# A two-layer trunk: layer 1's output projection as a seven-product stage behind the attention, and layer 0's weight sums and norm factors issued sooner

## The chip, the cores and the metric

One core of one Trainium2 chip runs the whole program. The metric is the device time of one execution in microseconds; the kernel before takes 1605.94 us, the median of three runs (1605.65 to 1606.53).

## What is computed

```python
def reference(x, norm_g, pool_w_in, pool_w, pool_scale, pool_w_out, sb_w_in, sb_w_out, norm_f):
    h = x                                        # (1, 1024, 1024) float32
    u = rms_norm(h, norm_g[0])                   # layer 0: pooling mixer
    xb, z = split(u @ pool_w_in, 2)              # 2048 channels each, 4 groups of 512
    pooled = [trailing_mean(xb[g], w) - xb[g] for g, w in enumerate((2, 4, 8, 16))]
    y = concat(pooled[g] @ pool_w[g]) * pool_scale * silu(z)
    h = h + y @ pool_w_out
    u = rms_norm(h, norm_g[1])                   # layer 1: stick-breaking attention
    q, k, v, z = split(u @ sb_w_in)              # 16 heads, q and k of 64, v of 128 columns
    a[t, s] = sigmoid(z_ts) * prod_{s<j<t} (1 - sigmoid(z_tj)),  s < t
    h = h + (concat(a @ v) * silu(z)) @ sb_w_out
    return rms_norm(h, norm_f)
```

All of it is float32. `sb_w_out` is 2048 x 1024.

## The kernel before

**Arithmetic.** Every float32 operand of a matmul is split into a high and a low part (`split`, L93: ACT copies the high part, DVE subtracts, L98 and L99), and a product is three matmuls (`mm3`, L87 to L91: high x high, high x low, low x high). `raw_of` (L102) loads an operand of 128 x 512 on SP's queue.

**Layer 0.** The input projection, and later the output projection, multiply 2 x 2 blocks of matrices with seven products instead of eight. That needs sums of blocks: sums of the weights on POOL (`sums`, L218), of the input on DVE, and of the results where the banks are read. `first_w` and the products `c1`, `c2` start it; `factors` (L176) loads the rows of x in 512 KB tiles, squares them on ACT and makes the root of the norm on POOL; `spread` (L187) turns it with PE and copies it; `to_u` (L195) scales x with it on DVE. Then four channel groups follow (`gi`, with windows of 2, 4, 8, 16). In each, `Group.rest` (L244) makes the branch and the gate in seven products, `pool_block` (L287) the window sums on DVE (L294, L297), and `mixed` (L305) the group's own matmul, the gate, and the y blocks: POOL puts y and its sums into DRAM (L321, L333 to L337). `out_sums` (L226) makes one of eight jobs of the output projection's weights: it loads four blocks into `a_raw` tiles (six buffers, which `Group.load` shares), adds four times on POOL, and puts four sums into DRAM from POOL's queue (L231, L233). The output projection is a stage of its own: `out_product` (L125) does one of its products in 8 blocks of 12 matmuls.

**Layer 1.** The attention goes by head, and in a head by slots of 256 queries. A slot's chain is: scores on PE (L714, L715), sigmoids on ACT (L719, L720), a mask on POOL (L723), a running product on DVE (L726), a product on DVE (L730), another mask on POOL (L733), transposes on PE (L758), splits on ACT and DVE (L761, L762), and the sum with v on PE; at the end of a query block DVE multiplies the gate in (L784). Between these steps `dense()` issues filler: pieces of the projections of q and k, z and v of the next heads (`qk_item`, `z_item`, `v_item`), and of the output projection (`out_item`, `out_proj`, L565). `QUANTA` and `order` say what is due in which head, and `rate` spreads it over the head's steps. The output projection takes a pair of heads at a time, with all eight products of blocks: for each of 8 row tiles and 2 column halves 6 matmuls over the pair, and an addition into `h` on DVE (L572). The last pair follows at the end, and `finish` (L674) makes the final norm of each row tile: two squares on ACT, three small steps on POOL (L115 to L119), two multiplications on DVE (L686), and the store.

**Order.** The program is written engine-neutral; a scheduler then sets the order of the instructions on each engine by its own estimate of their times, and tile pools hand out buffers, with waits where a buffer's last use is not over. What stands where on an engine is therefore read from the order, not from the code.

Of the kernel before, what the change touches and what calls it, by code (L numbers as in the profile page):

```python
# [15 lines left out]
P = 128  # L16
S = 1024
# [28 lines left out]
def trunk(ctx, tc, x, xt, g, pw, pg, psc, pwo, sqk, sv, sz, swo, nf, out):  # L46
# [38 lines left out]


# [53 lines left out]
    with tc.tile_pool(name="l0", bufs=2) as l0:  # L140
# [22 lines left out]

        def load_xt(k, l, n):
# [233 lines left out]
        firsts = [[xb_tile() for _ in range(2)], [l0.tile([P, S], F32, name="t0") for _ in range(2)]]  # L398
# [17 lines left out]

        for gi in range(len(WINDOWS)):
            pooled = {}
            for cp in range(2):
                if gi + cp:  # L420
                    dst = [xb_tile("old" if gi == 0 and i else "xb", 2 - (gi == 0 and i)) for i in range(2)]
                    Group(gi * 4 + 2 * cp).rest(dst, AF.Copy)
                    if gi > 1 and cp == 0:
                        out_sums((0, 7)[gi - 2])
# [4 lines left out]
            for op in range(2):  # L429
# [9 lines left out]
                if gi + op:  # L439
                    dst = [l0.tile([P, S], F32, name="t0") for _ in range(2)]  # L440
# [3 lines left out]
                if 0 < 2 * gi + op < 7:  # L444
# [9 lines left out]
    slots_ = ctx.enter_context(tc.tile_pool(name="slots", bufs=48, reuse_waits="tile"))  # L454
# [9 lines left out]


    with tc.tile_pool(name="ob", bufs=4, reuse_waits="tile") as ob:
        def operands(n):

            i, j = {1: (0, 0), 2: (0, 1), 4: (1, 1)}.get(n, (0, 0))

            def of(kb):
                w = wd[n][kb] if n in wd else pwo[8 * j + kb][:, i * 512:i * 512 + 512]
                return split(raw_of(w, ob)), split(raw_of(yd[n][kb], ob, "y_raw"), ob, "y")
# [5 lines left out]

        def rows(l):  # L480
            return range(4 * HALVES[l], 4 * HALVES[l] + 4)

        add = nc.gpsimd.tensor_tensor

        def masked(t, n, ps):
            if t < NT - 1:
                nc.vector.tensor_tensor(h[t, n], ps, h[t, n], ALU.add)
            else:
                nc.vector.scalar_tensor_tensor(
                    h[t, n], in0=ps, scalar=but_first, in1=h[t, n], op0=ALU.mult, op1=ALU.add)  # L490
# [69 lines left out]
    ps_d = ctx.enter_context(tc.tile_pool(name="ps_d", bufs=3, space=PSUM, reuse_waits="tile"))  # L560
    ps_q = ctx.enter_context(tc.tile_pool(name="ps_q", bufs=2, space=PSUM, reuse_waits="tile"))
    ps_t = ctx.enter_context(tc.tile_pool(name="ps_t", bufs=2, space=PSUM, reuse_waits="tile"))
    ps_o = ctx.enter_context(tc.tile_pool(name="ps_o", bufs=1, space=PSUM, reuse_waits="tile"))

    def out_proj(ys, w4, t):  # L565

        for n in range(2):
            po = ps_d.tile([P, 512], F32, name="pd")
            for i, (yh, yl) in enumerate(ys):
                wh, wl = w4[2 * i + n]  # L570
                mm3(po, yh, yl, wh, wl, i == 0, i == 1)
            nc.vector.tensor_tensor(h[t, n], po, h[t, n], ALU.add)  # L572


    with tc.tile_pool(name="l1", bufs=1, reuse_waits="tile") as l1:
        def load_w(*srcs):

            return [split(raw_of(src[:, c:c + 512], l1, bufs=4))
# [3 lines left out]
        qk, vt, gt, yt = {}, {}, {}, {}  # L582
# [27 lines left out]
        def z_item(head, halves=(1, 0)):  # L610
            w2 = load_w(sz[head])
            yield
            for half in halves:
# [7 lines left out]
                t1 = l1.tile([P, 512], F32, name="t1", bufs=4)  # L621
# [31 lines left out]
        o_w = {}  # L653

        def out_item(pr, pieces, last=False):
            if pr not in o_w:
                o_w[pr] = load_w(swo[2 * pr], swo[2 * pr + 1])
                yield
            for m in pieces:
                for tt in range(2):  # L660
                    ts_ = slice(tt * P, (tt + 1) * P)
                    ys = [(yt[2 * pr + a, m][0][:, ts_], yt[2 * pr + a, m][1][:, ts_]) for a in range(2)]
                    out_proj(ys, o_w[pr], 2 * m + tt)
                    if last:
                        finish(2 * m + tt)
                    yield

        nfb = []
        late_rows = []
        LATE_T = 6  # L670
        ended = []
        ov = out.rearrange("(t p) c -> t p c", p=P)

        def finish(t):  # L674
            if not nfb:
                for n in range(2):
                    b = l1.tile([P, 512], F32, name="w_raw", bufs=4)
                    nc.sync.dma_start(b, nf[:, n * 512:n * 512 + 512].broadcast_to([P, 512]))
                    nfb.append(b)
            if t < LATE_T and not ended:  # L680
                late_rows.append(t)
                return
            rs = rstd_of([h[t, 0], h[t, 1]])
            for n in range(2):
                cs = slice(n * 512, n * 512 + 512)
                nc.vector.scalar_tensor_tensor(  # L686
                    h[t, n], in0=h[t, n], scalar=rs, in1=nfb[n], op0=ALU.mult, op1=ALU.mult)
# [241 lines left out]
```

## Time and profile before

| | |
|---|---|
| median of three runs | 1605.94 us |
| the profiled execution, its own time | 1603.79 us |
| its span on the core | 1602.1 us |
| PE busy | 1545.7 us (96%) |
| DVE busy | 1135.7 us (71%) |
| ACT busy | 662.8 us (41%) |
| POOL busy | 412.5 us (26%) |
| mean granted clock of TensorE | 0.985 |
| chain that ended last | PE 72%, DVE 7%, DMA, ACT and POOL 1% each |

The span is cut in three: up to about 464 us layer 0's projection and pooling, to 633 us its output projection and the norm of layer 1, then the attention to 1583 us and the end. Times are of one profiled execution. An engine's busy time says little by itself: matmuls overlap, so a matmul's own length is longer than the step from one to the next.

### The profile page before, as it was taken

What the parts mean: (1) busy time and instruction counts of PE and PEld (TensorE: products, weight loads), DVE (VectorE), ACT (ScalarE), POOL (GpSimd) and SP (SyncE); (2) the same over time, 40 slices, a digit from 0 to 9 for tenths busy, and PEclk for the clock granted to TensorE, in tenths of its full rate; (3) what the DMA queues carried; (4) which work ended last, traced back from release to release, by engine and by line L of the source; (5) the groups of instructions that cost most, each with busy time, mean ns of one, the idle gap of its engine ahead of it and who ended that gap; (6) DMA issues with size and microseconds to landing.
All of it is one profiled execution on the core that took longest, in us unless ns stands there. A gap on an engine that the chain in (4) does not pass through costs nothing.

```text
span 1602.1 us, 23391 instructions
## 1 busy us (share of the span) xinstructions
PE 1545.7 (96%) x8256; PEld 1325.5 (83%) x8256; DVE 1135.7 (71%) x1681; ACT 662.8 (41%) x1310; POOL 412.5 (26%) x903
## 2 busy tenths in 40 slices
PE   7899999988989998999999999999999999999997
PEld 6677888866778886989889889889889889889886
DVE  6976957969945676477757757747757757757678
ACT  7432322212335464454435435435434434434444
POOL 0336465586440121111101101101101101101113
PEclk9899999998999998999999999999999999999999
DMA  8124352463468562111021021021021021021112
GB/s 309 33 69 156 105 184 103 149 222 138 147 242 294 183 200 72 56 57 41 27 66 41 27 66 40 27 66 40 28 66 41 27 66 40 28 66 40 33 42 106
DMA packets 75125, 149.92 MB, mean 94 GB/s; under 512 B 9728, under 2 KB 9728, under 8 KB 75008
## 3 DMA queue, kind: packets, MB, share of 16 engines
q1 hardware_dynamic: 67184, 123.25, 23.8%
q0 software_dynamic: 7680, 25.17, 4.2%
q8 instruction: 65, 1.06, 0.3%
q14 instruction: 52, 0.43, 0.1%
q10 hardware_dynamic: 144, 0.01, 0.0%
HBM read 110.64 MB, written 29.36 MB: 87 GB/s over the span
## 4 chain that ended last, share of the span: by engine, by line
PE 72%; DVE 7%; issue 1%; DMA 1%; ACT 1%; POOL 1%; SPq 0%; DVEq 0%; POOLq 0%; ACTq 0%
PE pd L89 15%; PE pd L91 15%; PE pd L90 15%; PE bk L89 4%; PE bk L90 4%; PE bk L91 4%; PE pt L758 4%; PE po L89 2%; PE po L90 2%; PE po L91 2%; PE pq L714 2%; PE pq L715 2%; DVE wsum L294 2%; DVE w_lo L99 1%; DVE wsum L297 1%
## 5 line engine op out<-in xcount | busy, mean ns | idle before, releaser
L726 DVE TENSOR_TENSOR_SCAN om<-om 128x257 f32<-128x257 f32 (+1 forms) x192 | 187.1, 979 | 80.3 <-POOL om L723 34.5
L99 DVE TENSOR_TENSOR w_lo<-w_raw,w_hi 128x512 fp32r<-128x512 f32 x214 | 157.0, 741 | 86.6 <-ACT w_hi L98 82.5
L89 PE MATMUL pd<-slot,w_hi 128*128 128x512 f32 x512 | 202.8, 396 | 4.1 <-DVE slot L542 4.0
L90 PE MATMUL pd<-slot,w_hi 128*128 128x512 f32 x512 | 201.7, 394 | 0.0
L91 PE MATMUL pd<-slot,w_lo 128*128 128x512 f32 x512 | 200.4, 392 | 0.0
L98 ACT ACTIVATE w_hi<-w_raw 128x512 fp32r<-128x512 f32 x214 | 133.6, 627 | 159.8 <-PE pd L90 75.9
L719 ACT ACTIVATE om<-pq 128x256 f32<-128x256 f32 (+1 forms) x192 | 94.4, 492 | 167.7 <-PE pq L715 161.9
L89 PE MATMUL pd<-w_hi,slot 128*128 128x256 f32 x512 | 146.4, 286 | 0.0
L723 POOL TENSOR_SCALAR_AFFINE_SELECT om<-om 128x128 f32<-128x128 f32 x128 | 49.2, 387 | 375.4 <-ACT om L719 373.1
L91 PE MATMUL pd<-w_hi,slot 128*128 128x256 f32 x512 | 144.5, 282 | 0.0
L90 PE MATMUL pd<-w_lo,slot 128*128 128x256 f32 x512 | 144.2, 282 | 0.0
L98 ACT ACTIVATE w_hi<-a_raw 128x512 fp32r<-128x512 f32 x88 | 53.7, 627 | 150.6 <-PE bk L90 57.4
L89 PEld LDWEIGHTS pd<-slot,w_hi 128*128 128x128 f32 x512 | 96.7, 189 | 22.4 <-DVE slot L542 4.3
L762 DVE TENSOR_TENSOR at_l<-pt,at_h 128x512 fp32r<-128x512 f32 (+1 forms) x160 | 99.6, 626 | 21.1 <-ACT at_h L761 20.8
L91 PEld LDWEIGHTS pd<-slot,w_lo 128*128 128x128 f32 x512 | 96.8, 189 | 19.9 <-DVE w_lo L99 0.4
L761 ACT ACTIVATE at_h<-pt 128x512 fp32r<-128x512 f32 (+1 forms) x160 | 86.7, 552 | 63.9 <-PE pt L758 63.2
L90 PEld LDWEIGHTS pd<-slot,w_hi 128*128 128x128 f32 x512 | 96.8, 189 | 18.1
L730 DVE TENSOR_TENSOR om<-pq,om 128x256 f32<-128x256 f32 (+1 forms) x192 | 104.8, 551 | 9.1 <-DVE om L726 0.5
L89 PE MATMUL pd<-w_hi,y_h 128*128 128x512 f32 x256 | 107.0, 418 | 0.4 <-ACT y_h L787 0.4
L90 PE MATMUL pd<-w_lo,y_h 128*128 128x512 f32 x256 | 102.2, 399 | 0.0
L91 PE MATMUL pd<-w_hi,y_l 128*128 128x512 f32 x256 | 100.4, 395 | 0.0
L718 POOL MEMSET om<- 128x1 f32 x192 | 18.0, 99 | 315.2 <-PE pt L758 210.1
(315 smaller groups left out, 4088.7 us busy)
## 6 DMA issues: line engine op xcount, KB each, us to landing
a_raw<-in_pw SPq DMA_DIRECT2D x64, 256.0 KB, 3.3
y_raw<-y_dram SPq DMA_DIRECT2D x52, 256.0 KB, 3.1
y_dram<-t POOLq DMA_DIRECT2D x48, 256.0 KB, 2.9
a_raw<-in_pwo SPq DMA_DIRECT2D x36, 256.0 KB, 2.7
w_raw<-in_sqk SPq DMA_DIRECT2D x34, 256.0 KB, 2.7
w_raw<-in_sz SPq DMA_DIRECT2D x34, 256.0 KB, 3.0
w_raw<-w_dram SPq DMA_DIRECT2D x32, 256.0 KB, 2.9
w_raw<-in_sv SPq DMA_DIRECT2D x32, 256.0 KB, 2.7
```

Of the source, the lines that this page charges most:

```text
L89: nc.tensor.matmul(ps, lhsT=lh, rhs=rh, start=start, stop=False, skip_group_check=more)
L90: nc.tensor.matmul(ps, lhsT=lh, rhs=rl, start=False, stop=False, skip_group_check=more)
L91: nc.tensor.matmul(ps, lhsT=ll, rhs=rh, start=False, stop=stop, skip_group_check=more)
L98: act(hi, raw, AF.Copy)
L99: nc.vector.tensor_tensor(lo, raw, hi, ALU.subtract)
L719: act(om[:, 1:1 + n], pz, AF.Sigmoid, scale=-ZSCALE)
L723: nc.gpsimd.affine_select(out=om[:, 1:1 + P], in_=om[:, 1:1 + P], pattern=[[1, P]], base=0, channel_multiplier=-1, compare_op=ALU.is_gt, f ...
L726: nc.vector.tensor_tensor_scan(out=om[:, :1 + n], data0=om[:, :1 + n], data1=om[:, :1 + n], initial=1.0 if s.first else carry[r], op0=ALU. ...
L730: nc.vector.tensor_tensor(om[:, :n], pz, om[:, :n], ALU.mult)
L758: nc.tensor.transpose(tp[:, c * P:(c + 1) * P], om[:, (j - b0) * P:(j - b0 + 1) * P], ident)
L761: act(ah[:, :n], tp[:, :n], AF.Copy)
L762: nc.vector.tensor_tensor(al[:, :n], tp[:, :n], ah[:, :n], ALU.subtract)
```

## The change

1. Layer 1's output projection becomes seven products of blocks, as in layer 0. The weights' sums are made in heads 1 to 8 (`w_load`, `w_sums`: four adds and four puts on POOL for each of 8 blocks). At the end of half a head, `y_half` puts y, and the sums of y, into DRAM from POOL's queue: one add and three puts for heads 0 to 7, three adds and five puts for heads 8 to 15. One product is filler in the last head (`first_product`); the other six, 576 matmuls, follow behind the attention, with PSUM banks and tiles of their own (`fin`).
2. With it go `out_item`, `out_proj`, the additions of L572, the splits of y (L787, L788), and the reversed order of the last head's query blocks. `w_raw` has 3 buffers instead of 4 there, `t1` 5 instead of 4, the slots are 52 instead of 48.
3. In layer 0, `factors` and the loads of the second half of x are issued between the two halves of `c1`, `spread(0)` within the second half, and three x tiles get buffers of their own; the jobs of `out_sums` are issued in the first three groups, none in the fourth.

```diff
...
+                if l == 0 or j == 3:
+                    t = wide(j)[:, :D]
+                else:
+                    t = l0.tile([P, S + 16], F32, name="old", bufs=1)[:, :D] if j == 0 else t0_tile()
                 nc.sync.dma_start(t, xv[4 * HALVES[l] + j])
...
             first_w(j)
+            if j:
+                factors(0)
+                factors(1)
+                for k in range(NK):
+                    load_xt(k, 1, (4, 3)[k // 4])
             for k in range(4 * j, 4 * j + 4):
+                if k == 6:
+                    spread(0)
                 for a, i in c1:
                     first_mm(c1[a, i], a, i, k, (1, 2))
-        factors(0)
-        factors(1)
-        for k in range(NK):
-            load_xt(k, 1, (4, 3)[k // 4])
-        spread(0)
...
+        JOBS = {(0, 1): 0, (1, 0): 4, (1, 1): 5, (2, 0): 6, (2, 1): 7}
...
-                    if gi > 1 and cp == 0:
-                        out_sums((0, 7)[gi - 2])
+                    if (gi, cp) in JOBS:
+                        out_sums(JOBS[gi, cp])
...
-                if 0 < 2 * gi + op < 7:
+                if gi == 0 and op or gi == 1:
                     out_sums(2 * gi + op)
...
+        def w_sums(kb):
+            a = w_a[kb]
+            s1 = l1.tile([P, 512], F32, name="w_raw", bufs=3)
+            add(s1, a[1, 0], a[1, 1], ALU.add)
+            add(a[1, 0], a[1, 0], a[0, 0], ALU.add)
+            yield
+            add(a[0, 0], a[0, 0], s1, ALU.add)
+            add(a[0, 1], a[0, 1], a[0, 0], ALU.add)
+            yield
+            for n, t in (5, s1), (7, a[1, 0]), (6, a[0, 0]), (3, a[0, 1]):
+                nc.gpsimd.dma_start(wd1[n][kb], t)
...
+        def put(n, kb, t):
+            nc.gpsimd.dma_start(yd1[n][kb], t)
+
+        def y_half(head, half):
+
+            j, kb = divmod(head, 8)
+            put(((0, 1), (3, 2))[j][half], kb, gt[head, half])
+            if half and j:
+                y_old[head] = [raw_of(yd1[n][kb], l1, "yo", bufs=2) for n in range(2)]
+            elif not half:
+                b = gt[head, 1], gt[head, 0]
+                if j == 0:
+                    t = l1.tile([P, 512], F32, name="yo", bufs=2)
+                    add(t, b[0], b[1], ALU.subtract)
+                    put(5, kb, t)
+                else:
+                    b12, b11 = y_old[head]
+                    add(b12, b[1], b12, ALU.subtract)
+                    put(7, kb, b12)
+                    add(b11, b12, b11, ALU.add)
+                    put(6, kb, b11)
+                    add(b[0], b11, b[0], ALU.subtract)
+                    put(4, kb, b[0])
...
-                order.append([va, (("o", pr - 1), out_item(pr - 1, (3, 2))), qb])
-                order.append([zb, (("o", pr - 1, 1), out_item(pr - 1, (1, 0)))])
+                order.append([(("p",), first_product())])
+        for kb in range(8):
+            order[1 + kb].insert(0, (("wl", kb), w_load(kb)))
+            order[1 + kb].append((("ws", kb), w_sums(kb)))
...
-        QUANTA = {"q": 9, "z": 9, "v": 9, "o": 9}
+        QUANTA = {"q": 9, "z": 9, "v": 9, "wl": 1, "ws": 2, "p": 24}
...
+        def operands(n):
+            def of(kb):
+                return (split(raw_of(w_plane(n, kb, swo, wd1), fin, bufs=6)),
+                        split(raw_of(yd1[n][kb], fin, "y_raw", bufs=6), fin, "y"))
...
+        pd = four()
+        out_product(pd, operands(5))
...
+        out_product(pb, operands(6))
...
+        out_product(pc, operands(7))
...
+        out_product(pc, operands(4), True)
...
+        out_product(pa, operands(2))
+        for i, t in enumerate(rows(0)):
+            masked(t, 0, pa[i])
+            finish(t)
...
+        for i, t in enumerate(rows(1)):
+            ts_ = slice(i * P, (i + 1) * P)
+            for kb in range(8):
+                (wh, wl), (yh, yl) = ops[kb]
+                mm3(pd[i], yh[:, ts_], yl[:, ts_], wh, wl, False, kb == 7, True)
+            nc.vector.tensor_tensor(h[t, 0], pd[i], h[t, 0], ALU.add)
+            finish(t)
```

The order of the instructions, which the scheduler sets, changes at three places as follows.

**The front, on DVE, before.** `g_..l` are the low parts of the second half of x (from `pl`, the loaded tiles), `L198` is `to_u`, and `t` and `xb` are gates and branches scaled with the norm factors.

```order
L162 SCALAR_TENSOR_TENSOR g_2l<-pl,g_sb,g_2h 128x512
L162 SCALAR_TENSOR_TENSOR g_3l<-pl,g_sb,g_3h 128x512
L162 SCALAR_TENSOR_TENSOR g_0l<-pl,g_sb,g_0h 128x512
L162 SCALAR_TENSOR_TENSOR g_1l<-pl,g_sb,g_1h 128x512
L162 SCALAR_TENSOR_TENSOR g_2l<-pl,g_sb,g_2h 128x512
L162 SCALAR_TENSOR_TENSOR g_3l<-pl,g_sb,g_3h 128x512
L99 TENSOR_TENSOR w_lo<-a_raw,w_hi 128x512
L198 SCALAR_TENSOR_TENSOR pl<-pl,g_sb,rsb 128x512 x8
L214 TENSOR_TENSOR t_571<-bk,rsb 128x512
```

The same place after the change (`L207` is `to_u`, `L223` the scaling):

```order
L165 SCALAR_TENSOR_TENSOR g_2l<-pl,g_sb,g_2h 128x512
L207 SCALAR_TENSOR_TENSOR pl<-pl,g_sb,rsb 128x512 x8
L223 TENSOR_TENSOR t_583<-bk,rsb 128x512
L165 SCALAR_TENSOR_TENSOR g_3l<-pl,g_sb,g_3h 128x512
L223 TENSOR_TENSOR t_584<-bk,rsb 128x512
L223 TENSOR_TENSOR xb<-bk,rsb 128x512
L165 SCALAR_TENSOR_TENSOR g_0l<-pl,g_sb,g_0h 128x512
L165 SCALAR_TENSOR_TENSOR g_1l<-pl,g_sb,g_1h 128x512
L165 SCALAR_TENSOR_TENSOR g_2l<-pl,g_sb,g_2h 128x512
L165 SCALAR_TENSOR_TENSOR g_3l<-pl,g_sb,g_3h 128x512
```

The eight rescalings have moved ahead of five of the eight low parts.

**The fourth channel group, on POOL, before.** `L221` to `L223` and `L276` are sums of a group's weights and of a job's, `L231` and `L233` a job's alone.

```order
L276 TENSOR_TENSOR a_raw<-a_raw 128x512
L221 TENSOR_TENSOR w_raw<-a_raw 128x512
L222 TENSOR_TENSOR a_raw<-a_raw 128x512
L233 DMA w_dram<-w_raw 128x512
L223 TENSOR_TENSOR a_raw<-a_raw,w_raw 128x512
L233 DMA w_dram<-a_raw 128x512
L221 TENSOR_TENSOR w_raw<-a_raw 128x512
L231 TENSOR_TENSOR a_raw<-a_raw 128x512
L233 DMA w_dram<-a_raw 128x512
L222 TENSOR_TENSOR a_raw<-a_raw 128x512
L233 DMA w_dram<-a_raw 128x512
L223 TENSOR_TENSOR a_raw<-a_raw,w_raw 128x512
```

The same place after the change (`L230` to `L232` and `L285` are a group's sums, `L330` and `L342` those of y):

```order
L293 MEMSET xb 128x16
L230 TENSOR_TENSOR w_raw<-a_raw 128x512
L231 TENSOR_TENSOR a_raw<-a_raw 128x512
L285 TENSOR_TENSOR a_raw<-a_raw 128x512
L293 MEMSET xb 128x16
L232 TENSOR_TENSOR a_raw<-a_raw,w_raw 128x512
L285 TENSOR_TENSOR a_raw<-a_raw 128x512
L330 DMA y_dram<-t_3239 128x512
L342 TENSOR_TENSOR old<-t_3239,old 128x512
```

Only the groups' own sums and y's steps are left there.

**The end of the attention, on ACT, before.** `at_h` are the attention's splits, `junk` the squares of the final norm.

```order
L761 ACTIVATE at_h<-pt 128x512
L787 ACTIVATE y_h<-t_15470 128x256
L113 ACTIVATE junk,ssq<-slot 128x512 x2
L761 ACTIVATE at_h<-pt 128x384
L787 ACTIVATE y_h<-t_15442 128x256
L113 ACTIVATE junk,ssq<-slot 128x512 x3
L787 ACTIVATE y_h<-t_15442 128x256
L113 ACTIVATE junk,ssq<-slot 128x512 x9
```

The same place on ACT after the change, with the semaphores that each row waits for (DMAHW are transfers of SP's queue, DMASW those of POOL's):

```order
L801 ACTIVATE at_h_14964<-pt_14959 128x512 [waits DVE_49,PE_49,Pool_49]
L101 ACTIVATE w_hi_15029<-w_raw_15027 128x512 [waits DMAHW0_49]
L101 ACTIVATE y_hi_15035<-y_raw_15033 128x512 [waits DMAHW1_49]
L101 ACTIVATE w_hi_15053<-w_raw_15051 128x512 [waits DMAHW2_49]
L101 ACTIVATE y_hi_15059<-y_raw_15057 128x512 [waits DMAHW3_49,DMASW7_49,Pool_49]
L101 ACTIVATE w_hi_15077<-w_raw_15075 128x512 [waits DMAHW4_49]
L101 ACTIVATE y_hi_15083<-y_raw_15081 128x512 [waits DMAHW5_49,DMASW4_49,DVE_49]
```

And on POOL the last puts and adds of y, of which the last put raises DMASW7:

```order
L707 DMA y3_dram1_127<-t1_14405 128x512 [waits DVE_49]
L723 TENSOR_TENSOR yo_14757<-t1_14405,yo_14757 128x512 [waits DMAHW4_49,DMASW0_49]
L707 DMA y7_dram1_131<-yo_14757 128x512 [waits DMASW5_49,Pool_49]
L725 TENSOR_TENSOR yo_14759<-yo_14757,yo_14759 128x512 [waits DMAHW5_49,DMASW1_49]
L707 DMA y6_dram1_130<-yo_14759 128x512 [waits Pool_49]
L727 TENSOR_TENSOR t1_14342<-yo_14759,t1_14342 128x512 [waits DMASW3_49]
L707 DMA y4_dram1_128<-t1_14342 128x512 [waits DMASW7_49,Pool_49]
```

The new stage's splits stand directly behind the attention's last one, and the second y_hi waits for POOL's last put.

## Rows read from the trace of the kernel before

**Rows 1.** The page, part 1: engines' busy us (share of the span) and instructions.
```profile
PE 1545.7 (96%) x8256; PEld 1325.5 (83%) x8256; DVE 1135.7 (71%) x1681; ACT 662.8 (41%) x1310; POOL 412.5 (26%) x903
```

**Rows 2.** Windows: length; busy us of PE, PEld, DVE, ACT, POOL; clock; DMA; GB/s.
```profile
12.00:30.00 18.00, 18.00 (x81) 14.87 (x81) 10.78 (x16) 14.18 (x23) 1.24 (x2) 1.00 1.05 395
250.00:300.00 50.00, 49.90 (x220) 40.86 (x219) 45.44 (x55) 16.71 (x29) 25.60 (x21) 1.00 0.32 111
350.00:400.00 50.00, 38.84 (x155) 30.49 (x154) 47.93 (x48) 11.09 (x20) 35.61 (x29) 0.90 0.42 146
359.60:366.40 6.80, 2.93 (x6) 1.82 (x6) 6.73 (x5) 2.71 (x5) 4.95 (x4) 0.50 0.32 117
400.00:440.00 40.00, 36.30 (x152) 29.20 (x152) 36.25 (x40) 13.17 (x23) 19.05 (x21) 0.96 0.43 149
720.00:1540.00 820.00, 820.00 (x4945) 727.08 (x4944) 563.47 (x901) 356.09 (x744) 118.75 (x495) 1.00 0.15 44
1540.00:1583.00 43.00, 41.44 (x231) 34.95 (x230) 38.17 (x65) 21.68 (x52) 9.29 (x33) 1.00 0.13 44
```

**Rows 3.** The page, part 5, one group of the old out projection.
```profile
L89 PE MATMUL pd<-w_hi,y_h 128*128 128x512 f32 x256 | 107.0, 418 | 0.4 <-ACT y_h L787 0.4
```

**Rows 4.** Timeline of PE, 351.76 to 363.06 us: start, length, instruction, idle before.
```profile
351.76 0.39 PE L90 MATMUL bk<-g_1l,w_hi 128*128 128x512 f32 x1
...
355.62 0.39 PE L91 MATMUL bk<-g_3h,w_lo 128*128 128x512 f32 x1
363.06 0.79 PE L89 MATMUL bk<-g_0h,w_hi 128*128 128x512 f32 x1 [7.05 <-ACT w_hi L98]
```

**Rows 5.** Timeline of POOL in layer 0: puts and adds of y.
```profile
453.32 1.19 POOL L321 DMA_DIRECT2D y_dram<-t  x2 [4.69 <-DVE t L314]
454.53 1.31 POOL L333 TENSOR_TENSOR old<-t,old 128x512 f32<-128x512 f32 x1
456.24 0.56 POOL L321 DMA_DIRECT2D y_dram<-old  x1 [0.41 <-POOL old L333]
```

**Rows 6.** The page, part 6: KB each, median us from issue to landing.
```profile
y_dram<-t POOLq DMA_DIRECT2D x48, 256.0 KB, 2.9
```

**Rows 7.** Timeline of ACT at the very end: the last square.
```profile
1595.46 0.63 ACT L113 ACTIVATE junk<-slot 128x512 bf16<-128x512 f32 x1
1596.00 0.19 ACT L113 ACTIVATION_READ_ACCUMULATOR junk<-slot 128x1 f32 x1
```

**Rows 8.** Waits of PE, 0 to 100 us: us in total, times, longest.
```profile
PE bk L191 <- POOL rs L185: 5.0, 1, 5.0
PE bk L89 <- ACT pl L302: 4.8, 1, 4.8
```

**Rows 9.** Timeline of DVE in the front.
```profile
31.70 5.39 DVE L198 SCALAR_TENSOR_TENSOR pl<-pl,g_sb,rsb 128x512 f32<-128x512 f32 x8 [3.57 <-ACT rsb L193]
```

**Rows 10.** Waits of PE, 340 to 470 us.
```profile
PE bk L89 <- ACT w_hi L98: 7.1, 1, 7.1
```

**Rows 11.** Timeline of POOL in the fourth channel group.
```profile
351.37 1.29 POOL L231 TENSOR_TENSOR a_raw<-a_raw 128x512 f32<-128x512 f32 x1
...
360.07 2.28 POOL L223 TENSOR_TENSOR a_raw<-a_raw,w_raw 128x512 f32<-128x512 f32 x1
```

**Rows 12.** Groups of DVE, 340 to 440 us: busy us, mean ns, idle before.
```profile
L99 DVE TENSOR_TENSOR w_lo<-a_raw,w_hi 128x512 fp32r<-128x512 f32 x21 | 21.2, 1029 | 0.8 <-ACT w_hi L98 0.8
L297 DVE SCALAR_TENSOR_TENSOR wsum<-wsum,xb 128x1024 f32<-128x1024 f32 x4 | 8.7, 2169 | 0.1
```

**Rows 13.** The same groups, 100 to 140 us.
```profile
L99 DVE TENSOR_TENSOR w_lo<-a_raw,w_hi 128x512 fp32r<-128x512 f32 x8 | 5.4, 683 | 6.1 <-ACT w_hi L98 6.1
...
L297 DVE SCALAR_TENSOR_TENSOR wsum<-wsum,xb 128x1024 f32<-128x1024 f32 x1 | 1.2, 1218 | 0.0
```

**Rows 14.** The page, part 5: scan and mask of the attention.
```profile
L726 DVE TENSOR_TENSOR_SCAN om<-om 128x257 f32<-128x257 f32 (+1 forms) x192 | 187.1, 979 | 80.3 <-POOL om L723 34.5
...
L723 POOL TENSOR_SCALAR_AFFINE_SELECT om<-om 128x128 f32<-128x128 f32 x128 | 49.2, 387 | 375.4 <-ACT om L719 373.1
```

More of the change, by code (lines that the diff above doesn't have):

```diff
@@ L84, in trunk @@
     wd = {n: dram.tile([8, P, 512], F32, name=f"w{n}_dram") for n in (3, 5, 6, 7)}
+    yd1 = {n: dram.tile([8, P, 512], F32, name=f"y{n}_dram1") for n in range(8)}
+    wd1 = {n: dram.tile([8, P, 512], F32, name=f"w{n}_dram1") for n in (3, 5, 6, 7)}
     def mm3(ps, lh, ll, rh, rl, start, stop, more=False):
@@ L397, in trunk @@
             u_split(6, kb, B[0, 0, kb])
-        firsts = [[xb_tile() for _ in range(2)], [l0.tile([P, S], F32, name="t0") for _ in range(2)]]
+        firsts = [[xb_tile() for _ in range(2)], [t0_tile() for _ in range(2)]]
         fns = AF.Copy, AF.Silu
@@ L439, in trunk @@
                 if gi + op:
-                    dst = [l0.tile([P, S], F32, name="t0") for _ in range(2)]
+                    dst = [t0_tile() for _ in range(2)]
                     Group(16 + gi * 4 + 2 * op).rest(dst, AF.Silu)
@@ L463, in load_h, with rows, masked, w_plane @@
         nc.sync.dma_start(h[t, n], xv[t][:, n * 512:n * 512 + 512])
+    def rows(l):
+        return range(4 * HALVES[l], 4 * HALVES[l] + 4)
+    add = nc.gpsimd.tensor_tensor
+    def masked(t, n, ps):
+        if t < NT - 1:
+            nc.vector.tensor_tensor(h[t, n], ps, h[t, n], ALU.add)
+        else:
+            nc.vector.scalar_tensor_tensor(
+                h[t, n], in0=ps, scalar=but_first, in1=h[t, n], op0=ALU.mult, op1=ALU.add)
+    def w_plane(n, kb, w, sums):
+        i, j = {1: (0, 0), 2: (0, 1), 4: (1, 1)}.get(n, (0, 0))
+        return sums[n][kb] if n in sums else w[8 * j + kb][:, i * 512:i * 512 + 512]
     with tc.tile_pool(name="ob", bufs=4, reuse_waits="tile") as ob:
         def operands(n):
-            i, j = {1: (0, 0), 2: (0, 1), 4: (1, 1)}.get(n, (0, 0))
             def of(kb):
-                w = wd[n][kb] if n in wd else pwo[8 * j + kb][:, i * 512:i * 512 + 512]
-                return split(raw_of(w, ob)), split(raw_of(yd[n][kb], ob, "y_raw"), ob, "y")
+                return (split(raw_of(w_plane(n, kb, pwo, wd), ob)),
+                        split(raw_of(yd[n][kb], ob, "y_raw"), ob, "y"))
             return of
@@ L668, in trunk @@
[L668 to L687, printed above, removed]
-                nc.sync.dma_start(ov[t][:, cs], h[t, n])
+        w_a = {}
@@ L784, in weighed @@
                 nc.vector.tensor_tensor(t1, po, t1, ALU.mult)
-                yh = l1.tile([P, 256], F32R, name="y_h", bufs=8)
-                yl = l1.tile([P, 256], F32R, name="y_l", bufs=8)
-                act(yh, t1, AF.Copy)
-                nc.vector.tensor_tensor(yl, t1, yh, ALU.subtract)
-                yt[s.head, s.p] = (yh, yl)
-                if s.head == NH - 1:
-                    queue.append((("o", NPAIR, s.p), out_item(pr, (s.p,), True)))
+                if s.p % 2 == 0:
+                    y_half(s.head, s.p // 2)
         order = []
@@ L836, in trunk @@
         for head in range(NH):
-            ps_ = (3, 2, 1, 0) if head < NH - 1 else (0, 1, 2, 3)
-            for p in ps_:
+            for p in (3, 2, 1, 0):
                 for gi, ks in enumerate(groups(p)):
```

131 lines of the change are left out of this document (86 added, 45 removed).

## The prediction

> **What bounds the kernel now.** I read the busy table first, then the windows by stage, then PE's waits in the stages that the change touches, then single timelines. The reader is to see in the busy table that PE works 1545.7 of 1602.1 us [rows 1], and in the windows where the missing 56 us are: between 720 and 1540 us, in the attention, PE is busy in all of its 820 us while DVE has 563 and POOL 119, so there only fewer matmuls make the kernel shorter [rows 2]. From 250 to 300 us PE is as good as full too, but from 350 to 440 us, the last channel group of layer 0, it stands still for (50 - 38.84) + (40 - 36.30) = 14.9 us while DVE has 47.93 of the first 50 [rows 2]. So the change has one part that takes work from a full engine and one that takes waits from a stage with holes. The profiled execution took 1603.79 us, 2.15 less than the median of 1605.94; the sum is made against 1603.79, and 2.15 are put back at the end. A measurement of this kernel tells a change from none at about 0.2%, 3.2 us.
>
> **Layer 1: the products.** The old out projection issues three groups of 256 matmuls of 512 columns, of which one is shown [rows 3]: 768. Seven products of 8 blocks with 12 matmuls make 7 x 96 = 672, so 96 go. The duration in that row (418 ns) is of pipelined instructions; the pace is the step from one start to the next: 351.76 to 355.62 us is 17 steps, 0.227 us each [rows 4]. So the products are worth 96 x 0.227 = **-21.8 us**, all of it on the path, since PE is full where they stood.
>
> What is added beside them lies on other engines. DVE loses 128 evictions and 64 y_l subtractions and gains 112 splits; ACT's copies change alike. POOL gets 32 adds for the weights and 8 + 24 for y, and 32 + 64 puts: at 1.31 and 0.56 us [rows 5] 84 + 54 = 138 us on top of 119 in 820. I cost that at nothing: PE's full 820 us hide it, and if that cover went, it is priced in the third rival. SP's new loads stand in a queue whose stage moves 44 GB/s [rows 2]: nothing.
>
> **Layer 1: the start of the new stage.** Here a wait is added. In the order of the change, ACT's y_hi for the second block of product 5 waits for a POOL semaphore and for the landing of the last y put, y4: its buffer takes the place of a tile that this put still reads. ACT and DVE are in order, so all later splits queue behind it, and PE, with 12 matmuls (2.7 us) of the first block, waits for them. Before y4 can start, POOL does, after the last attention product's eviction, put, add, put, add, put, add, put: 4 x 0.56 + 3 x 1.31 + 3 x 0.41 (the idle before a put that waits for its add) = 7.4 us [rows 5], and the put lands later; the median is 2.9 us [rows 6]. With the eviction and the first ACT copy (0.63, as long as a square [rows 7]) about 11.2 us pass, of which PE fills 2.7: **+8.5 us**. Bounds: 0, if the last heads' order lets POOL's chain run early, and 11. After a hole of 7.05 us the trace shows the granted clock at half, 1.2 GHz for 2.4, until 366.4, while PE worked from 363.06: 3.4 us at half pace, **+1.7** [rows 2, 4].
>
> Ahead of that the last head has the first product as its only filler, and in the order the last 55 rows of PE's attention are without it: some 8.6 us of PE work against DVE's chain for the last scores. I take 4.5 us of holes where the last head had 1.56 between 1540 and 1583 [rows 2] and near 0.5 later: **+2.5**, between 0 and +8. Product changes in the new stage, where all four banks' last products meet the splits of the next: **+1**, 0 to 3. The last rows: in the old order the square of one half ran while the other was evicted; now both squares follow the last eviction in ACT's order, one more of 0.63 + 0.19 [rows 7]: **+0.8**.
>
> **Layer 0: the front.** The two spreads, each ended by a POOL reciprocal root, cost PE 5.0 us in one wait, and the first group's pooling another 4.8 [rows 8]. The change loads x's tiles earlier, so the first of these waits should go. But three more x tiles of 512 KB then stand ahead of eight xt loads in SP's queue, about 4 us at the 395 GB/s of 12 to 30 us [rows 2], and in DVE's order the eight rescalings, 5.39 us [rows 9], now stand ahead of the fourth low part of the second half of x, which PE's next products need. Those 5.39 and an eviction and a split of some 0.7 each make 6.8 us, partly beside PE's first blocks. Bounds: -5 and +3. I take **-2**, since DVE's long string starts sooner by the wait it loses.
>
> **Layer 0: the weight sums.** Before, one job stood in the first channel group, two in the second, three in the third, two in the fourth; now two, four, two and none. In the fourth the longest wait is 7.1 us of PE for a w_hi [rows 10], whose POOL sum starts at 360.07. Of the job, one add and two puts stand behind the group's first sum and ahead of this one: 1.29 + 2 x 0.56 = 2.4 us [rows 11]; the rest of it holds four of six a_raw buffers. Without the jobs the hole should shrink by 2.4 at least, by 7.1 at most; I take 4, and half of the clock's 1.7. Beside POOL's adds DVE's w_lo takes 1.029 us and the last window sum 2.169 [rows 12], against 0.683 and 1.218 where POOL adds less [rows 13]. The jobs' eight adds are 8 x 1.29 = 10.3 us; a third of a w_lo's time there is stretch (0.346 of 1.029), so DVE, which bounds this stage, gets back 3.5. Sum: **-8.3**, between -3 and -13.
>
> The Trainium skill, "SBUF — State Buffer", section "Who interferes with whom", has it that a DVE instruction with two SBUF inputs and a GpSimd one that reads SBUF shut each other out for a whole instruction. By that rule the eight adds would give back their full 10.3 and not 3.5, and the time would be 1583. The trace's mean stretch, 0.35 us, is far from a whole add, so the sum stays with the rows; the first rival's second figure holds that case.
>
> In the second group two jobs more cost what a third job costs the third group: from 250 to 300 us PE has 49.90 of 50 with DVE at 45.44 [rows 2], so next to nothing; four may cost one hole. I take **+1.5**, 0 to +7.
>
> **Sum**: -21.8 + 8.5 + 1.7 + 2.5 + 1 + 0.8 - 2 - 8.3 + 1.5 = -16.1. 1603.79 - 16.1 + 2.15 = 1589.8, say **1590 us**.
>
> **Rivals.**
> 1. No wait at the new stage (chance 0.22). For: before, PE found work in the holes that the scheduler saw. Against: the order shows the wait. Without the 8.5 and 1.7 the time is 1580; with layer 0's fourth group at its bound as well (-4.7) 1575.
> 2. Layer 0 gives nothing (0.18): the holes only move, from the fourth group to the second, and in the front from the root to the low parts. For: DVE has 47.93 of 50 us in the fourth group anyway [rows 2], and jobs beside window sums stretch both. Then -8.8 is missing: 1599.
> 3. Slower: POOL becomes the wait of the attention (0.05). The three adds and four puts of y stand in POOL's queue among the masks of the next head's scores, and PE turns what the masks leave. Counted in the order of the change at the ends of heads 8, 10, 12 and 14, PE has 14.5 us of other work ahead of the third masked tile, which stands behind the whole chain: 4 x 0.56 + 3 x 0.41 + three adds, and then mask, scan, product and mask, 0.39 + 0.98 [rows 14] and about 1 for the other two. With adds of 2.28, as the second row of [rows 11] has one, that is 12.7 us, 1.8 to spare; at the odd heads' ends it is 18 of other work. It decides once an add takes over 2.9 us or waits as long for a load; at 5 us 6.4 are missing at each of four heads, with 1.7 for the clock: +32, so 1622.
> 4. The change does not take PE's time (0.07): the last head and the new stage turn out bound by DVE and ACT. Then the wait, the splits and the holes of the last head eat the products: +10 beyond the sum and layer 0 at half, 1604. Against it: the like stage of layer 0 is full.
>
> The Trainium skill's rule named above bears on the third rival: by it each add could hold DVE's scan for a whole add, 64 x 1.31 = 84 us in all. DVE has 257 us free in the attention [rows 2], so even by the rule that changes no term, and no row of this case shows a head with more than that.
>
> **How the numbers follow.** The forecast has 0.48: 1584 to 1596. The first two rivals are faster too, so faster by over 0.2% has 0.48 + 0.22 + 0.18 = 0.88, no change 0.07, slower 0.05. The range goes from the first rival with its bound, 1575, to the fourth rival, 1604; what is left out is the third rival and the tails of the others, less than 0.2.
>
> **What would show it.** Right: 672 matmuls of the out projection; windows of the attention with PE full; a wait of PE for ACT y_hi of some 8 us right after the last head, with the clock at half behind it; no wait of PE for w_hi over 5 us in the fourth group; in the front a wait on DVE's g low parts in place of the one on POOL. Wrong: waits of PE on the masked tiles at every head's end (third rival), a new stage with PE below nine tenths throughout (fourth), a fourth group as long as before (second), or a start of the new stage without a hole (first).

## The result, and the profile of the change

The prediction was wrong, and of the wrong sign. The change takes 1617.98 us, the median of four runs (1617.70 to 1620.24), against 1605.80 for the kernel before (four runs, 1605.54 to 1606.53): a ratio of 1.0078 with a 95% interval of 1.0061 to 1.0096, 12 us slower. The profiled execution has a span of 1616.1 us and a mean granted clock of 0.977, against 1602.1 us and 0.985.

The page, part 1, of the change, beside [rows 1]:

```profile
PE 1533.2 (95%) x8160; PEld 1311.6 (81%) x8160; DVE 1161.2 (72%) x1597; ACT 689.7 (43%) x1330; POOL 562.2 (35%) x1075
```

PE issues 96 matmuls fewer, as it should, but its busy time falls by 12.5 us and not by 21.8, and its idle time, span less busy, grows from 56.4 to 82.9 us. So the question is which new holes make 26.5 us, and where matmuls run at the lower clock. The windows of the change have the columns of [rows 2]:

```profile
157.00:170.00 13.00, 8.37 (x25) 5.91 (x25) 12.93 (x15) 4.49 (x8) 5.96 (x6) 0.74 0.42 140
250.00:300.00 50.00, 43.43 (x184) 35.14 (x183) 42.08 (x45) 11.09 (x20) 30.77 (x31) 0.93 0.44 146
350.00:400.00 50.00, 50.00 (x220) 40.97 (x219) 39.97 (x46) 12.53 (x21) 28.84 (x27) 1.00 0.45 148
440.00:480.00 40.00, 28.18 (x115) 22.26 (x113) 15.68 (x18) 5.50 (x10) 21.01 (x27) 0.91 0.43 150
476.30:496.70 20.40, 9.89 (x22) 7.29 (x23) 7.96 (x11) 6.96 (x12) 6.04 (x7) 0.50 0.80 271
480.00:600.00 120.00, 113.19 (x478) 92.79 (x479) 71.45 (x111) 57.66 (x107) 17.59 (x22) 0.93 0.71 233
700.00:1450.00 750.00, 749.79 (x4699) 671.57 (x4699) 554.72 (x794) 360.95 (x737) 263.60 (x696) 1.00 0.29 94
```

The attention is as full as before, though POOL has 263.60 us of work in it. The fourth channel group did what the prediction asked: PE has 50.00 of 50 us where [rows 2] have 38.84. But the second and third groups now have holes (250 to 300 us: 43.43 where [rows 2] have 49.90; from 140 to 300 us PE does 612 matmuls where the kernel before does 701), and the start of layer 0's output projection has a large one, behind which TensorE stays at 1.2 GHz up to 496.7 us. The same two windows there before:

```profile
440.00:480.00 40.00, 35.70 (x150) 28.95 (x149) 16.99 (x23) 11.75 (x20) 18.80 (x22) 0.96 0.66 238
480.00:600.00 120.00, 120.00 (x548) 99.84 (x547) 78.83 (x124) 61.48 (x115) 15.68 (x19) 1.00 0.71 228
```

The waits of PE name the places. For the change, 0 to 640 us (us in total, times, longest):

```profile
PE bk L92 <- ACT y_hi L101: 12.0, 1, 12.0
PE bk L92 <- DVE xb L269: 9.5, 3, 6.6
...
PE bk L92 <- DVE t L223: 4.2, 1, 4.2
PE bk L93 <- DVE g_3l L165: 3.9, 1, 3.9
...
PE bk L94 <- DVE w_lo L102: 2.7, 1, 2.7
PE bk L94 <- DVE y_lo L102: 2.4, 1, 2.4
```

Of these, only the 3.9 on `g_3l` was foreseen, in place of the 5.0 on `rs` [rows 8]. The wait for a w_hi [rows 10], 7.1 us, is gone. Behind the attention stands the wait that the prediction priced at 8.5 us:

```profile
PE fk L92 <- ACT y_hi L101: 7.5, 1, 7.5
```

### The profile page after: what moved, and what is told of

The parts are those of the page before. It is cut to its first block, busy times and chain, and to the rows that moved or that the text cites. A ratio compares the mean times of both kernels' runs of the same rounds, so it can differ in the third digit from the quotient of the medians.

```text
span 1616.1 us, 23745 instructions
## 1 busy us (share of the span) xinstructions
PE 1533.2 (95%) x8160; PEld 1311.6 (81%) x8160; DVE 1161.2 (72%) x1597; ACT 689.7 (43%) x1330; POOL 562.2 (35%) x1075
## 4 chain that ended last, share of the span: by engine, by line
PE 65%; issue 3%; DMA 2%; DVE 2%; POOL 2%; ACT 1%; DVEq 0%; POOLq 0%; ACTq 0%; SPq 0%
PE pd L92 11%; PE pd L94 11%; PE pd L93 11%; PE pt L798 4%; PE bk L94 3%; PE bk L93 3%; PE bk L92 3%; PE fk L92 3%; PE fk L93 3%; PE fk L94 2%; PE po L92 2%; PE po L93 2%; PE po L94 2%; PE pq L754 2%; PE pq L755 2%
## 5 line engine op out<-in xcount | busy, mean ns | idle before, releaser
L766 DVE TENSOR_TENSOR_SCAN om<-om 128x257 f32<-128x257 f32 (+1 forms) x192 | 215.4, 1124 | 84.8 <-POOL om L763 57.2
L102 DVE TENSOR_TENSOR w_lo<-w_raw,w_hi 128x512 fp32r<-128x512 f32 x222 | 177.3, 801 | 58.4 <-ACT w_hi L101 54.9
L92 PE MATMUL pd<-slot,w_hi 128*128 128x512 f32 x512 | 207.8, 406 | 2.3 <-ACT w_hi L101 2.3
L93 PE MATMUL pd<-slot,w_hi 128*128 128x512 f32 x512 | 202.0, 395 | 0.0
L101 ACT ACTIVATE w_hi<-w_raw 128x512 fp32r<-128x512 f32 x222 | 138.6, 625 | 138.0 <-PE pd L93 39.8
L102 DVE TENSOR_TENSOR y_lo<-y_raw,y_hi 128x512 fp32r<-128x512 f32 x92 | 66.2, 719 | 87.7 <-ACT y_hi L101 79.4
L101 ACT ACTIVATE y_hi<-y_raw 128x512 fp32r<-128x512 f32 x92 | 57.9, 629 | 124.4 <-PE bk L93 56.8
L773 POOL TENSOR_SCALAR_AFFINE_SELECT om<-om 128x128 f32<-128x128 f32 x128 | 54.2, 426 | 132.2 <-DVE om L770 132.2
L93 PEld LDWEIGHTS pd<-w_lo,slot 128*128 128x128 f32 x512 | 97.5, 190 | 0.8
L92 PEld LDWEIGHTS pd<-w_hi,slot 128*128 128x128 f32 x512 | 97.4, 190 | 0.6
```

Of the source, the lines that this page charges most:

```text
L92: nc.tensor.matmul(ps, lhsT=lh, rhs=rh, start=start, stop=False, skip_group_check=more)
L93: nc.tensor.matmul(ps, lhsT=lh, rhs=rl, start=False, stop=False, skip_group_check=more)
L101: act(hi, raw, AF.Copy)
L102: nc.vector.tensor_tensor(lo, raw, hi, ALU.subtract)
L766: nc.vector.tensor_tensor_scan(out=om[:, :1 + n], data0=om[:, :1 + n], data1=om[:, :1 + n], initial=1.0 if s.first else carry[r], op0=ALU. ...
L773: nc.gpsimd.affine_select(out=om[:, :P], in_=om[:, :P], pattern=[[1, P]], base=0, channel_multiplier=-1, compare_op=ALU.is_gt, fill=0.0)
```

## The experiments

The median of the kernel before lay between 1605.88 and 1606.98 us in the four sets of runs; each ratio is against the one of its own set, with its 95% interval.

**Which part costs: three parts of the change.** The first run has layer 1's change with layer 0 as before; the second adds the earlier factors, the third the new places of the jobs, each to the first.

```diff
-                    if (gi, cp) in JOBS:
-                        out_sums(JOBS[gi, cp])
+                    if gi > 1 and cp == 0:
+                        out_sums((0, 7)[gi - 2])
...
```

> The change in layer 1 alone; layer 0 as before. Theory A (the loss lies in layer 0, where the weight sums moved beside the window sums): layer 1 keeps its own gain, which by the two traces is 974.1 - 968.4 = 5.7 us, so about 1600 us. Theory B (the attention pays for POOL's new adds and puts, layer 0 is neutral): about as slow as the full change, 1612 to 1618 us.

> Layer 1's change and the norm factors sooner, the weight-sum jobs where they were. Theory A: the factors alone move little; the front lost 2 to 3 us in the trace of the full change, so 1600 to 1604 us, and the fourth channel group has its 7 us hole again. Theory C (the front's new order itself shifts everything behind it): above 1608 us.

> Layer 1's change and the weight-sum jobs in the first three groups, the factors where they were. Theory A: nearly all of the loss, 1613 to 1618 us, with holes of PE near 160 and 286 us, a fourth group without holes, and a hole of some 12 us with a long stretch at half clock at the start of layer 0's output stage. Theory C: 1600 to 1606 us.

Layer 1 alone took 1600.87 us, 0.9966 [0.9956, 0.9975]: 5.1 faster, where the prediction's terms of layer 1 make -7.3. With the factors it took 1606.39, 1.0000 [0.9989, 1.0010], so they cost 5.5; with the jobs 1612.36, 1.0049 [1.0033, 1.0066], so these cost 11.5. 1600.9 + 5.5 + 11.5 = 1617.9 is the change: the parts add up, and the loss comes with the two parts in layer 0.

**The wait at layer 1's new stage.** On layer 1 alone, the stage's four `x_` tiles are requested ahead of the first y_hi. The y_hi then lies elsewhere and has no put to wait for:

```diff
+                w = split(raw_of(w_plane(n, kb, swo, wd1), fin, bufs=6))
+                y = raw_of(yd1[n][kb], fin, "y_raw", bufs=6)
+                if not x_:
+                    x_.extend(fin.tile([P, 512], F32, name="x_") for _ in range(4))
+                return w, split(y, fin, "y")
...
```

> As the first run, with four result tiles of the last stage requested ahead of its y_hi tiles, so that no early y_hi takes the place of the tile of the last y put. If the wait for that put is what PE stands still for at the start of the stage, the hole of 7.5 us and the half clock behind it (1.7 us) go: 9 us less than the first run, about 1591 us. If the stage's start is late for another reason (loads, splits, DVE's end of the attention), 0 to 3 us less.

1590.79 us, 0.9911 [0.9892, 0.9930]. The wait is gone, and with it 10.1 us; the prediction had 8.5 and 1.7 for the clock. The longest of PE's waits that is left from 640 us to the end is:

```profile
PE po L92 <- ACT at_h L796: 1.6, 1, 1.6
```

**Why the factors cost 5.5.** In the second run, DVE's waits from 460 to 490 us, at the start of layer 0's output projection, have one that the prediction never looked for:

```profile
DVE y_lo L102 <- POOL t L346: 6.4, 1, 6.4
```

A y_lo of the new stage waits for POOL's last sum of y. The change requests `old` and a `t0` first in `factors`, and so they get lower places in SBUF (`old` at byte 151424 instead of 216960 of a partition, `t0` at 155584 instead of 208768), which overlap the places of the stage's y_hi (147072 to 155264) and y_lo (from there to 163456). It is the same kind of wait as at layer 1's stage. The next run has the factors sooner, on top of the run without layer 1's wait, and requests the stage's `xn` and `v` tiles ahead of its y_hi:

```diff
+                if not a1:
+                    xns.extend(ob.tile([P, 512], F32, name="xn", bufs=8) for _ in range(8))
+                    a1.extend(tmp2("v") for _ in range(4))
...
```

> On the fourth run: the norm factors sooner, with the jobs as before, and layer 0's output stage requests its xn and v tiles ahead of y_hi and y_lo, so that these no longer take the place of old and t0, to which the change gave lower addresses. Theory D (the factors' 5.5 us are that place: y_hi and y_lo of the stage's second block wait for the last y puts): as the fourth run or up to 2 us less, 1588 to 1591 us, and no wait of y_lo on a y put. Theory E (the front's own new order costs): 1596 us.

1591.59 us, 0.9909 [0.9894, 0.9923], beside 1590.79 without the factors: the 5.5 shrank to 0.8, which is no difference. So the places cost nearly all of the 5.5, and what issuing the factors sooner gives, a forecast 2, is not seen. This takes the new tile requests to be worth nothing on the kernel without the factors, where they were not run.

**Why the jobs cost 11.5: their place.** One theory said that a job hurts where it stands beside DVE's window sums. The next run, on top of the one without layer 1's wait, puts all jobs in the gate halves of the first three groups; another has the factors and the tile requests of the run above too.

```diff
+        GATES = {(0, 0): (0,), (0, 1): (1,), (1, 0): (2,), (1, 1): (3, 7), (2, 0): (4,), (2, 1): (5, 6)}
...
+                for kb in GATES.get((gi, op), ()):
+                    out_sums(kb)
```

> On the fourth run: all eight weight-sum jobs in the first three groups as in the change, but each behind a gate's products and none beside the window sums (which stand behind the branch's products). Theory A1 (the place beside the window sums made the holes): no hole over 4 us near 160 and 286 us, a fourth group without a hole; what is gained there, some 15 us, may be given back at the output stage's start as in the full change, so 1578 to 1591 us. Theory A2 (POOL simply has too much to do in the first three groups, wherever the jobs stand): holes there and 1598 to 1604 us.

> The fifth and sixth runs' edits together. If they are independent the differences add: between 1576 and 1591 us by the theories A1 and D, about 1605 us by A2 and E.

1612.65 us, 1.0033 [1.0020, 1.0046], and 1606.01, 1.0001 [0.9991, 1.0010]. The theory falls: the jobs cost 21.9 us there, more than in the change's places (the third group has three of them instead of two), and the stage's start still has its hole. PE's waits in the first of the two, 140 to 520 us:

```profile
PE bk L92 <- ACT y_hi L101: 11.8, 1, 11.8
PE bk L92 <- ACT w_hi L101: 7.2, 3, 4.1
PE bk L92 <- DVE t L266: 6.9, 1, 6.9
```

**Why the jobs cost 11.5: the queue ahead of the stage.** Back to the change. SP's queue, 456 to 492 us:

```profile
460.49 17.17 SPq L340 DMA_DIRECT2D old<-y_dram  x4
477.77 0.39 SPq L107 DMA_DIRECT2D w_raw<-in_pwo  x1
478.27 0.46 SPq L107 DMA_DIRECT2D y_raw<-y_dram  x1
```

And ACT behind it:

```profile
481.62 0.63 ACT L101 ACTIVATE w_hi<-w_raw 128x512 fp32r<-128x512 f32 x1 [15.47 <-DMA w_raw<-in_pwo]
483.72 0.63 ACT L101 ACTIVATE y_hi<-y_raw 128x512 fp32r<-128x512 f32 x1 [1.47 <-DMA y_raw<-y_dram]
484.42 0.63 ACT L101 ACTIVATE w_hi<-w_raw 128x512 fp32r<-128x512 f32 x1
489.79 0.63 ACT L101 ACTIVATE y_hi<-y_raw 128x512 fp32r<-128x512 f32 x1 [4.74 <-DMA y_dram<-old]
```

The four loads into `old`, which has one buffer, wait until the sums of the y block before are put away, and the operands of PE's next product stand behind them in the same queue. The last row's 4.74 us is the wait by tile place again. The kernel before stands there too, for 13.27 us, with a wait of PE of 4.3 on y_hi; but there the next load leaves the queue at 461.91 us, and in the change at 477.77, 15.9 later. The edit, on layer 1 without its wait and with the jobs of the change, moves the last two loads into `old` to POOL's queue:

```diff
-                    nc.sync.dma_start(o[:, n * 512:n * 512 + 512], yd[n][kb])
+                    (nc.gpsimd if kb == 7 else nc.sync).dma_start(o[:, n * 512:n * 512 + 512], yd[n][kb])
```

> Layer 1's change without the put wait, the jobs as in the change, the factors as before (third run's layer 0); the two loads into old for the last y block are issued from POOL's queue instead of SP's. Without this edit it would be 1612.4 - 10.1 = 1602 us. Theory F (the hole of 11.5 us at the start of layer 0's output stage is SP's queue standing before these loads, with the stage's own loads behind them): the hole shrinks to 2 to 4 us and the half clock behind it, 1590 to 1594 us. If the stage waits for the y values themselves, the hole stays, 1601 to 1604 us.

1593.92 us, 0.9919 [0.9902, 0.9936]. Without the edit, 1590.8 + 11.5 = 1602.3 was to be had, if those two add, so it gives 8.4. The queue stands 10.01 us instead of 17.17 and is free at 462.29, and PE's waits from 440 to 520 us, where the third run has 11.5 for y_hi, read:

```profile
PE bk L92 <- DVE t L220: 4.4, 1, 4.4
PE bk L92 <- ACT y_hi L101: 1.3, 1, 1.3
```

**Job by job.** With all three waits treated, `JOBS` was taken from the old places to those of the change in steps: none, job 7 from the fourth group to the second, then job 6 from the fourth to the first as well, then the change's whole table.

```diff
+        JOBS = {(2, 0): 0, (1, 1): 7}
```

> The fifth run and, from the eighth, the last two loads into old on POOL's queue; jobs as before the change. If SP's queue also holds up the output stage's start with the old jobs (holes of 4.3 to 8.5 us there in the runs so far), 3 to 8 us less than the fifth run: 1584 to 1589 us. If that hole waits for the y values, 1591 us again.

> The ninth run with one of the fourth group's two jobs (7) moved to the second half of the second group. If the hole of 7 to 9 us at 355 us comes from this job's adds and tiles, it goes with its half clock, 8 to 10 us; a hole of at most 9 us with its clock may come in the second group instead: 1577 to 1590 us. If POOL's load in the second group counts at all, nearer the upper end.

> The tenth run and job 6 moved from the fourth group to the first: one job more in each of the first two groups, three in the third, none in the fourth. If what a group can bear is two jobs in the first and three in the second, below the tenth run, 1574 to 1585 us; if every job ahead of the fourth group makes a hole as in the full change, 1590 to 1596 us.

> The full change, unaltered in jobs and factors, with the three repairs alone: x_ ahead of y_hi in layer 1's stage, xn and v ahead of y_hi in layer 0's, the last two loads into old on POOL's queue. If the three waits and the clock behind them are what the runs so far say (10.1, 5.5 and about 8.4 us), 1618 - 24 = 1594 us, and what is left over 1591 are the holes of the second and third group less the gain of the fourth. If they overlap, 1597 to 1604 us.

They took 1586.98 (0.9880 [0.9859, 0.9900]), 1592.60 (0.9911 [0.9894, 0.9929]), 1596.51 (0.9941 [0.9918, 0.9964]) and 1601.25 us (0.9971 [0.9960, 0.9982]); the last was expected at 1594. The cause of the 7 us above that lay in the treatment itself: `v`, which I had requested early (its first tile from byte 163456), came to lie on the end of a `t0` (159680 to 163776) that POOL still put from. ACT in that last run, 486 to 500 us:

```profile
489.56 0.64 ACT L101 ACTIVATE w_hi<-w_raw 128x512 fp32r<-128x512 f32 x1 [1.42 <-DMA w_raw<-w_dram]
498.14 1.57 ACT L516 ACTIVATE v<-bk 128x512 f32<-128x512 f32 x3 [7.95 <-DMA y_dram<-t]
499.59 0.64 ACT L101 ACTIVATE y_hi<-y_raw 128x512 fp32r<-128x512 f32 x1
```

The copy to `v` waits 7.95 us for a put, and a y_hi stands behind it. So three of these four were run once more with the stage's `x_` tiles requested early in the place of `v`:

> The ninth run with x_ in place of v requested early, as v then lay on the end of t0 (the twelfth run's ACT waits 8 us for the last y put before it copies into v). With the jobs as before the chain of y ends earlier and that wait hardly counts: 1584 to 1588 us.

> The tenth run with the same edit. Theory G (the fourth group is bound by DVE's window sums; without the job PE only does 48 matmuls of the output projection earlier, and the y blocks come no sooner): the hole of 6.5 us at the second product goes, some 8 us, and what is left is the second group's load, so 1585 to 1589 us, not clearly below the thirteenth run. Theory H (the moved job does shorten the fourth group, and only the wait for v hid it): 1576 to 1582 us.

> The twelfth run with the same edit: the full change with its three waits out of the way. If v's place made the twelfth run slower than the sum of the single repairs, 7 to 9 us less, 1592 to 1594 us; what then lies over the thirteenth run is what the moved jobs cost by themselves (theory G: 5 to 9 us; theory H: below zero). If not, 1601 us again.

1587.02 us (0.9878 [0.9863, 0.9892]) with the jobs where they were, **1585.21** (0.9864 [0.9849, 0.9878]) with one job moved, the best of all, though 1.8 is within the two intervals, and 1591.50 (0.9904 [0.9887, 0.9920]) for the whole change without its three waits. So without these waits the change takes 1618.0 - 1591.5 = 26.5 us less; one by one they measured 10.1 (layer 1's stage), 5.5 - 0.8 = 4.7 (the places in layer 0's stage) and 8.4 (the queue), 23 in all. Not all of that is the change's own loss: with the jobs where they were, the edit to the queue gave 1591.6 - 1587.0 = 4.6 too (fifth and ninth run), so about half of the queue's part was to be had without moving a job. With the waits gone, the new places of the jobs cost 4.5 (1591.5 against 1587.0).

## Why the prediction was wrong, point by point

Between the 16.1 us less that were forecast and the 12.2 more that were measured lie 28.3. The jobs have 18.3 of them (-6.8 forecast, +11.5 measured), the front 7.5 (-2 and +5.5) and layer 1 has 2.2 (-7.3 and -5.1).

**The products and layer 1: right.** 96 matmuls went and the attention stayed full, so the third rival, POOL as its wait, did not come about. The wait for the last put was 7.5 us where I had 8.5, and cost 10.1 with the clock where I had 10.2. The last head's waits are 1.6, 1.4, 1.1 and 0.8, 4.9 in all (I had 4.5). Layer 1 as a whole gave 5.1 of the 7.3 expected. Where the 2.2 went is not shown; single executions are no help there, as the same layer 0 has a wait of PE on y_hi of 8.5 us in the first run's profile and of 4.3 in the fourth's.

**The front: a gain of 2 that was none, and a cost of 5.5 that I did not look for.** The wait on `rs` gave way to one on `g_3l`, as said, and the rest cancelled. What failed is the step "Layer 0: the front" as a list: it followed the instructions that move, but not the tiles that they request first, though I had priced just such a wait in layer 1.

**The jobs: the step that failed most.** "Layer 0: the weight sums" had -8.3 in the fourth group and +1.5 in the second; the part measured +11.5. Three things were wrong in it.

First, the hole of 7.1 us in the fourth group was not on the path. It did close, but the group became no shorter. DVE's last window sum of the third group and that of the fourth, before:

```profile
304.51 1.22 DVE L297 SCALAR_TENSOR_TENSOR wsum<-wsum,xb 128x1024 f32<-128x1024 f32 x1
418.81 1.23 DVE L297 SCALAR_TENSOR_TENSOR wsum<-wsum,xb 128x1024 f32<-128x1024 f32 x1
```

The same two in the change:

```profile
317.04 1.22 DVE L306 SCALAR_TENSOR_TENSOR wsum<-wsum,xb 128x1024 f32<-128x1024 f32 x1
431.92 1.23 DVE L306 SCALAR_TENSOR_TENSOR wsum<-wsum,xb 128x1024 f32<-128x1024 f32 x1
```

From one to the other it is 114.3 us before and 114.9 in the change, though PE does 495 matmuls in that time and not 412. PE filled its holes with work that it had not done in the groups ahead: up to 440 us it has started 1695 matmuls, before 1703. And the group starts 12.5 us late, so its y blocks, and the loads of the stage behind them, come late too, and PE has no other work left meanwhile: it waits 4.2 and 12.0 us at the stage's start. In the prediction the fourth group's end was taken for PE's; the row with DVE at 47.93 of 50 [rows 2] spoke against it, and I used it only for the second rival. That DVE ends the group is not shown either: in the change it is busy for 39.97 of 50 us, and the group is as long.

In the two comparable runs, jobs as before and one job moved, it is the same on a smaller scale. The windows, in this order:

```profile
350.00:400.00 50.00, 37.86 (x146) 29.38 (x145) 46.51 (x47) 10.50 (x19) 35.32 (x29) 0.86 0.42 138
440.00:470.00 30.00, 29.46 (x125) 23.69 (x124) 10.51 (x16) 9.17 (x15) 14.23 (x18) 0.97 0.59 205
```

```profile
350.00:400.00 50.00, 47.08 (x197) 37.68 (x197) 47.95 (x53) 14.07 (x24) 33.50 (x30) 0.97 0.48 160
440.00:470.00 30.00, 23.32 (x92) 18.10 (x92) 11.88 (x15) 8.48 (x14) 14.89 (x18) 0.89 0.63 221
```

With the job moved PE does 197 matmuls instead of 146 in the first window, and then 92 instead of 125 in the second. The last window sums:

```profile
420.31 1.22 DVE L306 SCALAR_TENSOR_TENSOR wsum<-wsum,xb 128x1024 f32<-128x1024 f32 x1
```

```profile
423.25 1.23 DVE L306 SCALAR_TENSOR_TENSOR wsum<-wsum,xb 128x1024 f32<-128x1024 f32 x1
```

Those of the third group start at 303.61 and 309.18 us. So the fourth group is 2.6 us shorter here, where the prediction had 8.3 for two jobs, and it starts 5.6 later. PE did matmuls of the first output product early, and then had fewer to lay over the last y blocks.

Second, the cost in the second and third groups was not 1.5: the third group's last window sum is 12.5 us later than before. POOL works through its queue in order, and a group's own sum there stands behind a job's. POOL in the change, 145 to 165 us, and ACT, which needs the sum:

```profile
155.39 1.31 POOL L240 TENSOR_TENSOR a_raw<-a_raw 128x512 f32<-128x512 f32 x1
156.63 0.56 POOL L242 DMA_DIRECT2D w_dram<-a_raw  x1
157.21 2.11 POOL L232 TENSOR_TENSOR a_raw<-a_raw,w_raw 128x512 f32<-128x512 f32 x1
```

```profile
159.35 1.15 ACT L101 ACTIVATE w_hi<-a_raw 128x512 fp32r<-128x512 f32 x2 [12.83 <-POOL a_raw L232]
```

PE's holes of 1.9 and 2.7 us that follow, with the clock at 0.74 from 157 to 170 us, are the kind of hole that left the fourth group. The third group has one of 6.6 us on `xb`, with DVE's window sums ahead of it.

Third, the stretch of DVE moved along and was not all saved. From 140 to 300 us a w_lo takes 1031 ns where the kernel before has 887 (view by group; the change):

```profile
L102 DVE TENSOR_TENSOR w_lo<-a_raw,w_hi 128x512 fp32r<-128x512 f32 x37 | 37.7, 1031 | 1.0 <-ACT w_hi L101 1.0
```

In the fourth group, between the window sums above, the 24 instructions of DVE that write `wsum` take 39.9 us before and 31.8 in the change, so 8.1 came back, where I had 3.5; the w_lo there take 997 ns each in both. By the rule of the Trainium skill ("SBUF — State Buffer", "Who interferes with whom") the prediction had 10.3; the measurement lies between, and neither figure reached the end of the kernel.

**The rivals and the chances.** Rival 2, that layer 0 gives nothing, was nearest: it had the holes move from the fourth group to the second, and they moved to the second and third. But it put the worst case at zero. No rival had layer 0's output stage start with a new wait, though the rows at 440 to 480 us could have shown one (35.70 of 40); I did not follow the gain into the stage behind the one that was to get faster. The chance of 0.05 for slower rested on one mechanism in the attention, where the profile had room, and the range of 1575 to 1604 was too narrow by the same omission.

**What stays open.** What sets the length of the fourth group is not shown. Whether the 4.5 us of the jobs' new places are POOL's order or DVE's stretch was not separated; the jobs' puts on another queue were not tried.

## What to carry to other kernels

When the holes of an engine in a stage are to be filled, ask first whether the stage then ends sooner, and look at the queue at the start of the stage behind: here the fourth group took 114.3 us with PE's holes and 114.9 without, and work that PE does early no longer covers a wait later. When a change requests tiles sooner or in another order, list which later tiles fall on their places, at every stage, not only at the one that is new; a request moved by some lines was worth about 4.7 and 10.1 us here. A load into a tile with one buffer holds back everything behind it in its queue, so its place in the queue is to be costed as a wait.

## What was not expected of the hardware

After a hole of 12.03 us PE worked again from 484.40 us, with another hole of 2.41 at 488.2, and the granted clock was 0.50 up to 496.70 us, for 12.3 us from the restart. In the third run the hole at the same place is 11.51 us long with none behind it, and PE works from 486.57 us; the stretch at half clock there:

```profile
478.50:492.10 13.60, 5.53 (x13) 4.38 (x14) 5.78 (x8) 4.85 (x8) 6.23 (x8) 0.50 0.92 315
```

That is 5.5 us from the restart, and the sixth and seventh run, with holes of 11.82 and 11.57 us, have 5.5 and 5.7. Behind the 7.05 us hole of [rows 4] it was 3.4 us, and in layer 1 a hole of 7.5 us cost 10.1. So a second hole close behind the first costs more than its own length: this one fell while the clock was still low, and some 7 us more passed at 1.2 GHz.
